# Tile-by-tile ends of two output projections, later S5 set-up in layer 1, and small products ordered behind large ones, in a two-layer decoder trunk

## Chip, cores and metric

The kernel runs on one core of one Trainium2 chip, in one launch. The metric is device microseconds (us) of that core for one execution; the time of a kernel is the median over its runs. Engines are named as in the profile: PE is TensorE (PEld its weight loads), DVE is VectorE, ACT is ScalarE, POOL is GpSimd, SP is SyncE, which here only starts transfers.

## What is computed

The reference runs two layers over x (256 tokens, 1024 channels) and 256 memory tokens, all in float32:

```python
for l in range(2):
    x = x + 0.5 * swiglu(rms_norm(x, ffn1_norm[l]), ...)        # FFN1, width 2816
    h = rms_norm(x, mix_norm[l])
    z = h @ w_in[l]                                             # columns for 4 mixers + 4 gates
    y_a, y_b, y_c, y_d = mlstm(...), s5(...), gla(...), rwkv7(...)
    merged = sum(sigmoid(gate_b) * y_b)                         # per channel
    x = x + merged @ w_out[l]
    x = x + cross_attention(rms_norm(x, xattn_norm[l]), rms_norm(mem, mem_norm[l]))   # ends in @ wo
    x = x + 0.5 * swiglu(rms_norm(x, ffn2_norm[l]), ...)        # FFN2
return rms_norm(x, final_norm)
```

S5 is a complex diagonal state-space model of 32 groups; GLA is gated linear attention with 4 heads, whose scores are built here in eight levels (block sizes 128, 64, ... 1). The rest of the reference is not touched by the change.

## The kernel before

**Layout.** Activations lie transposed, 128 channels on the partitions and 256 tokens along the free axis; `self.x` is 8 such tiles. Each large product is made in float32 out of two rounded parts: weight w is split into hi and lo (`whi`, `wlo`), the activation too (`xhi`, `xlo`), and `mm3` (L256) adds three products hi*hi, hi*lo, lo*hi into PSUM. The FFN's later tiles use `mm2` (L263), one 512-column and one 256-column matmul per block.

**Weights.** `chunk` (L229) fetches 128x1024 halves in the order in which they are first used: a transfer on SP's queue into one of 3 `wraw` buffers, a copy to `whi` on ACT (L244), a subtraction to `wlo` on DVE (L245). There are 4 `whi`/`wlo` buffers; a buffer is free again when its 8 blocks' matmuls (24 of `mm3`) are done.

**Order of the work.** Only SP's queue keeps the order of the program text. The other engines' queues are put in order at build time by a list scheduler that simulates the program: an engine takes, among the instructions that are ready in the simulation, the one that stands first in the text. On the chip each queue then runs strictly in that order, and an instruction that is not ready holds up all behind it. `tc.issue_after(i)` adds the rule that what is written inside the block stands behind instruction i in the queue of i's engine; it adds no wait for i to end.

**FFN1 and S5's set-up.** `ffn` (L396) has 22 steps f (gate and up columns) and 8 steps d (down). In FFN1 it calls `s5_ahead` (L445) after each step with numbers 0 to 29. At the numbers in `S5_AT[layer]` POOL's share of S5's set-up is written (`s5_prep`, L1054, then `s5_mats`, L1152, for tiles 0 to 3: 49 small POOL instructions each, which build Bp and Cp); at the numbers in `S5_PE[layer]` the rest of a tile follows (`s5_finish`, L460): 8 transposes (L1209), 8 products (L1215, two instructions each in the trace), three ACT copies (L1210, L1218), four DVE instructions (L1220) and six transfers on ACT's queue (L1225, L1228).

```python
S5_AT = (2, 6, 11, 17, 22), (3, 8, 13, 18, 22)
S5_PE = (17, 22, 25, 29), (14, 19, 24, 28)
```

**The mixer stage.** `mix` (L647) writes RWKV first and then interleaves four generators by the string `ORDER[layer]`: S is one step of S5, G of GLA, M of mLSTM, D of the dense work (16 gate steps `gps`, 48 matmuls of `mm3` each in two halves of 24, L1576 and L259 to L261, in `gates`, L1564; then the keys and values of the memory). The third G to the tenth are GLA's eight levels: DVE differences (L785, L786), an ACT exponential (L787), three POOL products (L788, L794 or L798), then the score matmuls (L804, L807 or L810) and their copy into A (ACT L814, L817, or DVE L822). `gQ` has two buffers, used by turns. An S5 tile (`s5_tile`, L1254) multiplies into `px` (L1262) and `yps` (L1265), scans on DVE, adds the outputs into `yps` (L1290), then applies its nonlinearity.

**The projections.** `mix_out` (L1624, w_out) and the end of `xattn` (L520, wo) both call `proj_k` (L598) for four input chunks c: for each of 8 output tiles d it adds 6 matmuls into `acc`, and at c = 3 DVE adds the finished tile to `self.x` (L610). The next product's inputs are made from x by `gained` (ACT L343 `xhi`, DVE L344 `xlo`), and its norm from squares (ACT L310, POOL L312). In `xattn` chunk c is head c; `head(3)` is written between chunks 0 and 1.

Of the kernel before, what the change touches and what calls it, by code (L numbers as in the profile page):

```python
# [18 lines left out]
P = 128  # L19
# [5 lines left out]
LAZY = 5, 5  # L25
MEM_AT = 0, 0
S5_AT = (2, 6, 11, 17, 22), (3, 8, 13, 18, 22)
S5_PE = (17, 22, 25, 29), (14, 19, 24, 28)
ORDER = ("SSDSSSDSSSGSDSSGSDSGDGDGDGDGDGDDGDGDGMDGMDGMMDMDMMDMDDDDDD",
         "SSSSSSSSSSSSDSDGDGDGDMGDMGDMGDMGDMGDMGDMGDMGDGDGDDDDDDDDDD")  # L30
POS = 0, 1, 3, 2, 4
# [45 lines left out]
class K:  # L77
# [173 lines left out]
    def split(self, src, hi, lo, scale=None, eng=None):  # L251
        nc = self.nc
        nc.scalar.copy(hi, src)
        (eng or nc.vector).tensor_tensor(lo, src, hi.bitcast(F32), ALU.subtract)

    def mm3(self, ps, w, x, first, last):  # L256

        nc = self.nc
        nc.tensor.matmul(ps, w[0], x[0], start=first, stop=False)  # L259
        nc.tensor.matmul(ps, w[0], x[1], start=False, stop=False)  # L260
        nc.tensor.matmul(ps, w[1], x[0], start=False, stop=last)  # L261

    def mm2(self, ps, w, x, first, last):  # L263

# [255 lines left out]
    def xattn(self):  # L520
        nc, l = self.nc, self.l
        self.pdt = "psd", 2
        if self.kv is None:
            self.mem_gained()
            for _ in self.mem_kv():
                pass
        (kT, v), self.kv = self.kv, None
        self.br = "x"
        hi, lo = self.gained(self.x, "xattn_norm")
        qs, acc = [], [self.px([P, 2, T], "acc", br="o") for _ in range(4)]  # L530

        def q_of(c):
            ps = self.pd("qps")
            self.prod(self.chunk(self.ins["wq"][l, c]), ps, hi, lo, c == 0)
            qT = [self.hp.tile([P, 2, T], F32R, name=self.nm("qT")) for _ in range(2)]
            self.split(ps, *qT)
            qs.append(qT)
        for c in range(2):
            q_of(c)
        y = self.rstd_tok(self.x)  # L540
        rq = self.tp.tile([P, 4], F32, tag="rq", name=self.nm("rq"))
        nc.vector.tensor_scalar(rq[:, 0:2], y, 1.0 / 16, None, ALU.mult)
        nc.vector.tensor_scalar(rq[:, 2:4], y, -1.0 / 16, None, ALU.mult)
        es = [self.softmax(0, qs, rq, kT)]
        q_of(2)
        es.append(self.softmax(1, qs, rq, kT))
        oh = [self.head(0, es[0], v)]
        q_of(3)
        for h in range(2, 4):
            es.append(self.softmax(h, qs, rq, kT))  # L550
            oh.append(self.head(h - 1, es[h - 1], v))
        self.proj_k("wo", 0, *oh[0], acc)
        oh.append(self.head(3, es[3], v))
        for h in range(1, 4):
            self.proj_k("wo", h, *oh[h], acc)

    def softmax(self, h, qs, rq, kT):

# [36 lines left out]
        self.split(ops, hi, lo)  # L595
        return hi, lo

    def proj_k(self, wname, c, hi, lo, acc):  # L598

        nc, l = self.nc, self.l  # L600
        blk = self.chunk(self.ins[wname][l, c])
        for d in range(8):
            ps = acc[d // 2][:, d % 2, :]
            for k in range(2):
                w = blk(2 * d + k)
                for i, (wi, x) in enumerate(((0, hi), (0, lo), (1, hi))):
                    nc.tensor.matmul(ps, w[wi], x[:, k, :], start=(c == 0 and d % 2 == 0 and k == 0 and i == 0),  # L607
                                     stop=(c == 3 and k == 1 and i == 2), skip_group_check=True)
            if c == 3:
                nc.vector.tensor_tensor(self.x[:, d, :], ps, self.x[:, d, :], ALU.add)  # L610


    def ot(self, shape, dt=F32, n="ot", bufs=None):
# [99 lines left out]
    def gla(self):  # L713
        nc, l, sp = self.nc, self.l, self.tp
        self.small_cols()
        ps = self.wtiles(7)
        q = self.ot([P, 2, T], n="cq")
        nc.scalar.mul(q, ps, 0.125)
        ps = self.wtiles(8)
# [3 lines left out]
        for c in range(2):  # L723
            blk = self.chunk(self.ins["cv"][l, c])
            ps = self.pd("vps")
# [12 lines left out]
        ps = self.px([P, 2, T])  # L738
# [13 lines left out]
        b = self.ot([P, 2, T], n="gb")  # L752
# [19 lines left out]
        for tt in range(2):  # L772
            for pr in range(2):
                for par in range(2):
                    c = 4 * tt + 2 * pr + par
                    nc.scalar.mul(A[:, pr, tt, par, :], self.ident, dg[:, c:c + 1])
        yield
        for lv, m in enumerate((128, 64, 32, 16, 8, 4, 2, 1)):
            nb = 2 * T // (2 * m)
            halves = lambda t: f2(t).rearrange("p (n h j) -> p n h j", h=2, j=m)  # L780
            bv = halves(b)
            X = self.ot([P, 2, T], n="gE", bufs=3)
            Xv = halves(X)
            mid = bv[:, :, 0, m - 1:m].to_broadcast([P, nb, m])
            nc.vector.tensor_tensor(Xv[:, :, 0, :], mid, bv[:, :, 0, :], ALU.subtract)  # L785
            nc.vector.tensor_tensor(Xv[:, :, 1, :], bv[:, :, 1, :], mid, ALU.subtract)  # L786
            nc.scalar.activation(X, X, AF.Exp, scale=1.0 / 16)  # L787
            nc.gpsimd.tensor_tensor(Xv[:, :, 0, :], Xv[:, :, 0, :], halves(k)[:, :, 0, :], ALU.mult)  # L788
            Qm = Q[:, lv % 2]
            for par in range(2):  # L790
                r = slice(64 * par, 64 * par + 64)
                if m == 128:
                    second = lambda t: halves(t)[r, :, 1, :].rearrange("p a (g j) -> p a g j", j=64)
                    nc.gpsimd.tensor_tensor(Qm[r, :, par, :].rearrange("p (a g) j -> p a g j", a=2), second(X), second(q),  # L794
                                            ALU.mult)
                else:
                    second = lambda t: halves(t)[r, :, 1, :].rearrange("p (a n) j -> p a n j", a=4)
                    nc.gpsimd.tensor_tensor(Qm[r, :, par, :].rearrange("p a (n j) -> p a n j", j=m), second(X), second(q),  # L798
                                            ALU.mult)
            ps = self.px([P, 4, 2, 64])  # L800
            for c in range(4):
                pr, tt = divmod(c, 2)
                if m == 128:
                    nc.tensor.matmul(ps[:, c], X[:, pr, 0:P], Qm[:, c], start=True, stop=True)  # L804
                elif m >= 32:
                    for n in range(0, P, 2 * m):
                        nc.tensor.matmul(ps[n:n + m, c, :, 0:m], X[:, pr, tt * P + n:tt * P + n + m],  # L807
                                         Qm[:, c, :, n // 2:n // 2 + m], start=True, stop=True)
                else:
                    nc.tensor.matmul(ps[:, c], X[:, pr, tt * P:(tt + 1) * P], Qm[:, c], start=True, stop=True)  # L810
            pu = ps.rearrange("p c a t -> p (c a) t")
            if m == 128:
                for pr in range(2):
                    nc.scalar.copy(Ao[:, pr].rearrange("p a (g t) -> p g a t", t=64), ps[:, 2 * pr:2 * pr + 2])  # L814
            elif m >= 32:
                for n in range(0, P, 2 * m):
                    nc.scalar.copy(Au[n:n + m, :, n + m:n + 2 * m], pu[n:n + m, :, 0:m])  # L817
            else:

                half = lambda ap: ap.rearrange("p (n h j) -> p n h j", h=2, j=m)[:, :, 1, :]  # L820
                mask = half(self.lvl[m].bitcast(I32)).unsqueeze(1).to_broadcast([P, 8, P // (2 * m), m])
                nc.vector.copy_predicated(Au.rearrange("p u (n h j) -> p u n h j", h=2, j=m)[:, :, :, 1, :], mask,  # L822
                                          pu.rearrange("p u (n j) -> p u n j", j=m))
            yield
# [3 lines left out]
        for pr in range(2):  # L828
            ops = self.px([P, 2, T])
            for par in range(2):  # L830
                h = 2 * pr + par
# [5 lines left out]
            for par in range(2):  # L837
                for tt in range(2):
                    sq = ops[:, tt, par * P:(par + 1) * P]
                    c = tt * 4 + 2 * pr + par  # L840
# [12 lines left out]
        for hp in range(2):  # L853
            ps = self.wtiles(9 + hp)
# [4 lines left out]
            for hh in range(2):  # L859
                h = hp * 2 + hh  # L860
# [393 lines left out]
    def s5_tile(self, i, us, y):  # L1254

        nc, l, sp = self.nc, self.l, self.tp
        V = nc.vector.tensor_tensor
        W, In, Cp = self.Wp[i], self.In[i], self.Cp[i]
        w = self.px([P, 2, T])
# [3 lines left out]
        yps = self.px([P, 4, P], n="yps", br="y")[:, :, 0:64]  # L1263
# [21 lines left out]
        ss = a  # L1285
        V(ss[:, 0, :], a[:, 0, :], b[:, 1, :], ALU.subtract)
        V(ss[:, 1, :], a[:, 1, :], b[:, 0, :], ALU.add)
        for j in range(4):
            for ri in range(2):
                nc.tensor.matmul(yps[:, j, 1:64], Cp[:, j, ri].rearrange("p a b -> p (a b)"),  # L1290
                                 ss[:, ri, 64 * j:64 * j + 63], start=False, stop=(ri == 1), skip_group_check=True)
        yield
        th = self.ot([P, T], n="bth", bufs=1)
        tv = th.rearrange("p (j k) -> p j k", k=64)
# [329 lines left out]
    def mix_out(self):  # L1624
        nc, l = self.nc, self.l
        m = self.merged
        self.tap(f"merged_{l}", m)
        acc = [self.px([P, 2, T], "acc", br="o") for _ in range(4)]
        for c in range(4):
            hi = self.ot([P, 2, T], F32R, n="mghi")  # L1630
            lo = self.ot([P, 2, T], F32R, n="mglo")
            sl = slice(2 * c, 2 * c + 2)
            nc.scalar.mul(hi, m[:, sl, :], 0.5)
            nc.vector.scalar_tensor_tensor(lo, m[:, sl, :], 0.5, hi.bitcast(F32), ALU.mult, ALU.subtract)
            self.proj_k("wout", c, hi, lo, acc)


    def final(self):
# [152 lines left out]
```

## Time and profile before

| | |
|---|---|
| median of 3 runs | 1828.23 us (1826.98 to 1835.68) |
| the profiled execution's own time | 1828.79 us |
| its span, first to last instruction | 1827.1 us |
| busy share of the span | PE 97%, PEld 91%, DVE 74%, ACT 53%, POOL 31% |
| mean granted TensorE clock | 0.986 |

A duration in the rows is that of one instruction from start to end; consecutive matmuls overlap, so PE is idle only where the profile shows a gap, with the engine that ended it in brackets. The granted clock is 1.00 at 2.4 GHz and 0.50 at 1.2 GHz.

### The profile page before, as it was taken

How to read it: one execution, taken by the hardware profiler on the slowest of the kernel's cores; microseconds unless marked ns; L12 is line 12 of the kernel's file. 1: busy time of each engine (PE TensorE's matmuls, PEld its weight loads, DVE VectorE, ACT ScalarE, POOL GpSimd, SP SyncE). 2: the span in 40 equal slices, each digit the busy share in tenths (PEclk: the TensorE clock that was granted, in tenths of full speed). 3: DMA queues.
4: the chain of work that ended last, by engine and by line, in shares of the span. 5: the costliest groups of instructions: out<-in, count | busy, mean ns of one | idle time of the engine just before them, and what ended most of it. 6: DMA issues, size and time to landing. Idle time of an engine off the chain costs nothing. (4 is left out here: it accounts for less than half of the span.)

```text
span 1827.1 us, 34052 instructions
## 1 busy us (share of the span) xinstructions
PE 1771.7 (97%) x13156; PEld 1657.4 (91%) x13156; DVE 1343.1 (74%) x2325; ACT 959.6 (53%) x1594; POOL 573.9 (31%) x765
## 2 busy tenths in 40 slices
PE   7999999999999999999999899999999999999997
PEld 7888899889999999988898789999989999999886
DVE  8987678895576876866699666698856667768654
ACT  4665464456454455555456454645555544546552
POOL 4999521170011211200149893113021103111001
PEclk9999999999999999999999899999999999999999
DMA  6575563457346653555557466635444586445553
GB/s 196 169 211 183 187 206 110 138 179 222 115 153 222 227 188 115 180 189 185 183 167 218 139 188 201 201 108 172 164 137 146 186 258 217 149 136 186 185 186 103
DMA packets 131843, 320.16 MB, mean 175 GB/s; under 512 B 45792, under 2 KB 50912, under 8 KB 131168
## 3 DMA queue, kind: packets, MB, share of 16 engines
q1 hardware_dynamic: 83664, 290.31, 49.6%
q10 hardware_dynamic: 48016, 27.67, 5.3%
q8 instruction: 103, 1.69, 0.4%
q14 instruction: 60, 0.49, 0.1%
HBM read 300.11 MB, written 16.52 MB: 173 GB/s over the span
## 5 line engine op out<-in xcount | busy, mean ns | idle before, releaser
L245 DVE TENSOR_TENSOR wlo<-wraw,whi 128x1024 fp32r<-128x1024 f32 x524 | 677.8, 1295 | 315.7 <-ACT whi L244 310.1
L244 ACT CAST whi<-wraw 128x1024 fp32r<-128x1024 f32 x524 | 547.2, 1048 | 575.7 <-issue 103.3
L266 PE MATMUL gu<-hl,whi 128*128 128x512 f32 x1024 | 363.4, 399 | 0.0
L267 PE MATMUL gu<-hl,wlo 128*128 128x256 f32 x1024 | 288.5, 282 | 0.4 <-DVE wlo L245 0.4
L266 PE MATMUL dn<-ahl,whi 128*128 128x512 f32 x704 | 248.4, 397 | 0.0
L266 PEld LDWEIGHTS gu<-hl,whi 128*128 128x128 f32 x1024 | 193.0, 189 | 47.5
L312 POOL TENSOR_TENSOR arena<-arena 128x256 f32<-128x256 f32 x69 | 75.2, 1090 | 483.2 <-ACT arena L310 480.3
L267 PE MATMUL dn<-ahl,wlo 128*128 128x256 f32 x704 | 197.2, 281 | 0.8 <-DVE wlo L245 0.8
L267 PEld LDWEIGHTS gu<-hl,wlo 128*128 128x128 f32 x1024 | 194.1, 190 | 0.9 <-DVE wlo L245 0.9
L266 PEld LDWEIGHTS dn<-ahl,whi 128*128 128x128 f32 x704 | 131.9, 188 | 31.6
L259 PE MATMUL gps<-hhi,whi 128*128 128x256 f32 x512 | 153.2, 299 | 6.2 <-ACT gst L1576 5.8
L260 PE MATMUL gps<-hlo,whi 128*128 128x256 f32 x512 | 150.5, 294 | 0.0
L261 PE MATMUL gps<-hhi,wlo 128*128 128x256 f32 x512 | 149.5, 293 | 0.8 <-DVE wlo L245 0.8
L267 PEld LDWEIGHTS dn<-ahl,wlo 128*128 128x128 f32 x704 | 133.0, 189 | 1.4 <-DVE wlo L245 1.1
L259 PE MATMUL zin<-hhi,whi 128*128 128x256 f32 x384 | 111.6, 291 | 2.4 <-ACT gst L1576 2.4
L260 PE MATMUL zin<-hlo,whi 128*128 128x256 f32 x384 | 110.5, 288 | 0.0
L259 PEld LDWEIGHTS gps<-hhi,whi 128*128 128x128 f32 x512 | 102.1, 199 | 9.2 <-ACT gst L1576 6.7
L261 PE MATMUL zin<-hhi,wlo 128*128 128x256 f32 x384 | 110.2, 287 | 0.0
L260 PEld LDWEIGHTS gps<-hlo,whi 128*128 128x128 f32 x512 | 101.9, 199 | 2.3 <-issue 2.0
L261 PEld LDWEIGHTS gps<-hhi,wlo 128*128 128x128 f32 x512 | 101.5, 199 | 1.7 <-DVE wlo L245 1.0
L261 PE MATMUL gu<-xhi,wlo 128*128 128x256 f32 x320 | 91.3, 285 | 0.1
L259 PE MATMUL gu<-xhi,whi 128*128 128x256 f32 x320 | 91.3, 285 | 0.0
(535 smaller groups left out, 4622.2 us busy)
## 6 DMA issues: line engine op xcount, KB each, us to landing
wraw<-in_gu_dram SPq DMA_DIRECT2D x176, 512.0 KB, 3.7
wraw<-in_dn_dram SPq DMA_DIRECT2D x88, 512.0 KB, 3.5
wraw<-in_win_dram SPq DMA_DIRECT2D x68, 512.0 KB, 4.0
wraw<-in_gates_dram SPq DMA_DIRECT2D x64, 512.0 KB, 4.2
gd<-gst ACTq DMA_DIRECT2D x32, 256.0 KB, 2.1
wraw<-in_wk_dram SPq DMA_DIRECT2D x16, 512.0 KB, 3.8
wraw<-in_wv_dram SPq DMA_DIRECT2D x16, 512.0 KB, 3.5
gld<-gd SPq DMA_DIRECT2D x32, 256.0 KB, 4.2
```

The source lines that it names most:

```text
L244: nc.scalar.copy(hi, raw)
L245: nc.vector.tensor_tensor(lo, raw, hi.bitcast(F32), ALU.subtract)
L259: nc.tensor.matmul(ps, w[0], x[0], start=first, stop=False)
L260: nc.tensor.matmul(ps, w[0], x[1], start=False, stop=False)
L261: nc.tensor.matmul(ps, w[1], x[0], start=False, stop=last)
L266: nc.tensor.matmul(ps, w[0], x, start=first, stop=False, skip_group_check=True)
L267: nc.tensor.matmul(ps[:, 1, :], w[1], x[:, 0, :], start=False, stop=last, skip_group_check=True)
L312: nc.gpsimd.tensor_tensor(acc, acc, sq, ALU.add)
```

## The change

It does four things. `proj_last` takes chunks 2 and 3 of both projections together, so that each output tile gets its last 12 matmuls and is then finished; c = 0 and c = 1 stay as they were. `S5_PE` of layer 1 moves the four `s5_finish` calls from 14, 19, 24, 28 to 17, 22, 26, 29. GLA's score matmuls and S5's output matmuls are put behind `self.large`, the last matmul of `mm3` written before them. `mix_out` makes all four input parts before the last two chunks.

```diff
-S5_PE = (17, 22, 25, 29), (14, 19, 24, 28)
+S5_PE = (17, 22, 25, 29), (17, 22, 26, 29)
...
+    def behind(self):
+
+        return self.tc.issue_after(self.large.ins)
+
     def mm3(self, ps, w, x, first, last):
...
-        nc.tensor.matmul(ps, w[1], x[0], start=False, stop=last)
+        self.large = nc.tensor.matmul(ps, w[1], x[0], start=False, stop=last)
...
         oh.append(self.head(3, es[3], v))
-        for h in range(1, 4):
-            self.proj_k("wo", h, *oh[h], acc)
+        self.proj_k("wo", 1, *oh[1], acc)
+        self.proj_last("wo", oh[2], oh[3], acc)
...
-    def proj_k(self, wname, c, hi, lo, acc):
+    def proj_k(self, wname, c, hi, lo, acc, ds=range(8), blk=None):
 
         nc, l = self.nc, self.l
-        blk = self.chunk(self.ins[wname][l, c])
-        for d in range(8):
+        blk = blk or self.chunk(self.ins[wname][l, c])
+        for d in ds:
...
+    def proj_last(self, wname, x2, x3, acc):
+
+        blks = [self.chunk(self.ins[wname][self.l, c]) for c in (2, 3)]
+        for d in range(8):
+            for c, x in ((2, x2), (3, x3)):
+                self.proj_k(wname, c, *x, acc, (d,), blks[c - 2])
...
             ps = self.px([P, 4, 2, 64])
-            for c in range(4):
...
+            with self.behind():
+                for c in range(4):
...
-        for j in range(4):
-            for ri in range(2):
-                nc.tensor.matmul(yps[:, j, 1:64], Cp[:, j, ri].rearrange("p a b -> p (a b)"),
-                                 ss[:, ri, 64 * j:64 * j + 63], start=False, stop=(ri == 1), skip_group_check=True)
+        with self.behind():
+            for j in range(4):
+                for ri in range(2):
+                    nc.tensor.matmul(yps[:, j, 1:64], Cp[:, j, ri].rearrange("p a b -> p (a b)"),
+                                     ss[:, ri, 64 * j:64 * j + 63], start=False, stop=(ri == 1), skip_group_check=True)
...
         acc = [self.px([P, 2, T], "acc", br="o") for _ in range(4)]
+        parts = []
         for c in range(4):
...
-            self.proj_k("wout", c, hi, lo, acc)
+            parts.append((hi, lo))
+            if c < 2:
+                self.proj_k("wout", c, hi, lo, acc)
+        self.proj_last("wout", *parts[2:], acc)
```

## Rows read from the trace of the kernel before

**Rows 1.** The page's first part: busy time, share of the span and instructions of each engine.

```profile
PE 1771.7 (97%) x13156; PEld 1657.4 (91%) x13156; DVE 1343.1 (74%) x2325; ACT 959.6 (53%) x1594; POOL 573.9 (31%) x765
```

**Rows 2.** PE's waits over the whole span: us in total, times, longest.

```profile
PE wps L1209 <- POOL s5Bp L1179: 7.8, 1, 7.8
...
PE gps L259 <- ACT gst L1576: 5.8, 5, 3.2
...
PE qps L261 <- DVE wlo L245: 1.9, 2, 1.0
...
PE qps L372 <- DVE xlo L344: 1.3, 4, 0.4
```

**Rows 3.** Windows: a plain FFN step; tile 0's stretch, layers 1, 0: busy, PEclk, DMA.

```profile
996.19:1001.84 5.65, 5.65 (x34) 4.79 (x32) 5.39 (x9) 3.27 (x6) 5.65 (x8) 1.00 0.90 280
1001.84:1020.40 18.56, 10.73 (x58) 8.96 (x57) 8.84 (x8) 2.58 (x5) 18.56 (x46) 0.72 0.22 66
121.43:129.21 7.78, 7.78 (x59) 6.79 (x57) 6.16 (x12) 4.12 (x9) 7.78 (x14) 1.00 0.73 189
```

**Rows 4.** PE's timeline: transposes of tiles 0 and 1 (layer 0), tile 0 (layer 1).

```profile
121.43 0.60 PE L1209 MATMUL wps<-consts,s5Bp 128*128 128x128 f32 x4
...
153.13 0.60 PE L1209 MATMUL wps<-consts,s5Bp 128*128 128x128 f32 x4
...
1009.82 1.32 PE L1209 MATMUL wps<-consts,s5Bp 128*128 128x128 f32 x4 [7.83 <-POOL s5Bp L1179]
```

**Rows 5.** POOL's timeline: first instruction and last memset of set-up tiles, both layers.

```profile
80.62 1.39 POOL L1187 TENSOR_TENSOR bu<-s5Bp,arena 128x128 f32<-128x128 f32 x1
...
116.48 0.52 POOL L1201 MEMSET s5box<- 128x512 f32 x1
...
147.09 0.52 POOL L1201 MEMSET s5box<- 128x512 f32 x1
...
979.31 1.39 POOL L1187 TENSOR_TENSOR bu<-s5Bp,arena 128x128 f32<-128x128 f32 x1
...
1043.25 0.40 POOL L1187 TENSOR_TENSOR bu<-s5Bp,arena 128x128 f32<-128x128 f32 x1 [7.61 <-DMA s5Bp<-in_s_bc_dram]
```

**Rows 6.** Timeline, layer 1: first matmul of w_out on PE, its last input part on DVE.

```profile
1534.57 0.28 PE L607 MATMUL acc<-mghi,whi 128*128 128x256 f32 x1
...
1543.14 0.68 DVE L1634 SCALAR_TENSOR_TENSOR mglo<-merged,mghi 128x512 fp32r<-128x512 f32 x1
```

**Rows 7.** PE's waits at the start of FFN2, windows 720 to 735 and 1620 to 1632.

```profile
PE gu L372 <- DVE xlo L344: 1.5, 2, 1.2
...
PE gu L372 <- DVE xlo L344: 1.2, 1, 1.2
```

**Rows 8.** DVE's timeline at the end of wo, layer 1: head 3's part, first finished tile.

```profile
1615.24 0.68 DVE L254 TENSOR_TENSOR olo<-ops,ohi 128x512 fp32r<-128x512 f32 x1
1618.13 0.43 DVE L610 TENSOR_TENSOR x<-acc,x 128x256 f32<-128x256 f32 x1 [2.21 <-PE acc L607]
```

**Rows 9.** Windows, columns as in rows 3: after wo (layer 1); GLA's levels (layer 0).

```profile
1626.90:1630.30 3.40, 3.40 (x19) 3.40 (x18) 3.15 (x3) 0.47 (x2) 3.17 (x4) 0.50 0.29 73
...
391.99:394.51 2.52, 0.00 (x2) 0.00 (x1) 2.49 (x5) 1.94 (x3) 2.46 (x1) 1.00 0.00 0
394.60:398.10 3.50, 3.50 (x17) 3.50 (x18) 3.43 (x5) 0.42 (x1) 3.42 (x3) 0.51 0.93 268
...
376.00:412.00 36.00, 32.15 (x264) 31.48 (x264) 35.42 (x53) 16.26 (x29) 25.03 (x20) 0.95 0.56 186
```

**Rows 10.** Gate matmuls (one of three) before L807's last group, L810's end, layer 1's L804.

```profile
L259 PE MATMUL gps<-hhi,whi 128*128 128x256 f32 x88 | 27.4, 311 | 3.2 <-ACT gst L1576 3.2
...
L259 PE MATMUL gps<-hhi,whi 128*128 128x256 f32 x160 | 49.3, 308 | 4.6 <-ACT gst L1576 4.6
...
L259 PE MATMUL gps<-hhi,whi 128*128 128x256 f32 x56 | 17.4, 310 | 0.0
```

**Rows 11.** PE's group of score matmuls of levels 3 to 7, window 376 to 412.

```profile
L810 PE MATMUL px<-gQ,gE 128*128 128x128 f32 x38 | 6.0, 283 | 2.5 <-POOL gQ L798 2.5
```

More of the change, by code (lines that the diff above doesn't have):

```diff
@@ L800, in gla @@
             ps = self.px([P, 4, 2, 64])
-            for c in range(4):
[L802 to L810, printed above, removed]
+            with self.behind():
+                for c in range(4):
+                    pr, tt = divmod(c, 2)
+                    if m == 128:
+                        nc.tensor.matmul(ps[:, c], X[:, pr, 0:P], Qm[:, c], start=True, stop=True)
+                    elif m >= 32:
+                        for n in range(0, P, 2 * m):
+                            nc.tensor.matmul(ps[n:n + m, c, :, 0:m], X[:, pr, tt * P + n:tt * P + n + m],
+                                             Qm[:, c, :, n // 2:n // 2 + m], start=True, stop=True)
+                    else:
+                        nc.tensor.matmul(ps[:, c], X[:, pr, tt * P:(tt + 1) * P], Qm[:, c], start=True, stop=True)
             pu = ps.rearrange("p c a t -> p (c a) t")
```

## The prediction, made before the changed kernel was run

> **What bounds the kernel now.** I read the page's busy shares first: PE is busy 97% of the span [rows 1], so the time is the sum of PE's work and of what holds it up. PE's waits come next [rows 2]. Leaving out the start and the end of the kernel, which the change does not touch, the list is short: one wait of 7.8 us for POOL in S5's set-up, 5.8 us in five waits of gate products for ACT, 3.2 us at the first query product (1.9 + 1.3), 2.5 us for POOL at GLA's scores [rows 11], and 2.7 us at FFN2's start [rows 7]. Then I looked at the windows for the granted clock: after a wait it falls to 0.50 for some us [rows 9], so a wait costs more than its own length. No instruction of PE disappears with this change, and none is added. Everything it can win is in these waits and the clock behind them.
>
> The sum is made against the profiled execution's 1828.8 us. The median of the runs is 0.6 us lower, and I take that off at the end. About 0.5% (9.1 us) is what a measurement of this kernel can tell from no change.
>
> **S5's set-up in layer 1.** The transposes of tile 0 stand behind step 14 and wait 7.83 us for POOL [rows 4]. The same work in layer 0 stands behind step 17 and does not wait. From tile 0's place to the start of the second FFN step after it, PE issues the same instructions in both layers (58 and 59 recorded), in 7.78 us at full clock in layer 0 and in 18.56 us at a mean clock of 0.72 in layer 1 [rows 3]. The difference, 10.8 us, is wait and half clock together. With 17 for 14, layer 1 has layer 0's place.
>
> Is POOL done by then? In layer 0 tile 0 took POOL from 80.62 to 116.48, 35.9 us, and PE came at 121.43, 4.9 us later [rows 4, 5]. In layer 1 POOL starts at 979.31, so by layer 0's pace it ends at 1015.2. PE would arrive three steps after 1001.84. A plain step is 5.65 us [rows 3], so it comes at 1018.8, 3.6 us after POOL. Tile 1 follows POOL in layer 0 by 6.0 us (147.09, 153.13) [rows 4, 5]. In layer 1 it takes POOL to 1015.2 + 30.6 = 1045.8, and PE comes at step 22, near 1051. Tile 2 waits in layer 1 for its input transfer, 7.61 us [rows 5]. That transfer is issued behind step 18, and steps now come 10.8 us sooner, so it lands before POOL is free at 1045.8. Tiles 2 and 3 then have eight us and more. The three copies on ACT, the four instructions on DVE and the six transfers on ACT's queue move along with each tile, past the weight copies of three FFN steps; they are inside layer 0's 7.78 us. I take **10.8 us**. Above it lies the same with a little of the mixer's first waits covered by tile 3's work, 11.6; below it the wait comes back in part, which is a rival.
>
> One rule speaks against this. The rows show the same POOL instruction at 1.39 us and at 0.40 us [rows 5]. During the wait DVE had little to do (8.84 us busy in 18.56) [rows 3], and POOL ran at its short times. The Trainium skill, "SBUF — State Buffer", section "Who interferes with whom", says that a DVE instruction with two SBUF inputs and a GpSimd instruction that reads SBUF exclude each other, the later one blocking. By that rule the chain that ended at 1009.8 was quick only because PE's wait had starved DVE, and it will be slower once the wait is gone; layer 0 shows by how much, 35.9 us, and that is the pace taken above.
>
> **The end of w_out, two layers.** A matmul of a dense product takes 0.12 us of PE (264 in 32.15 us [rows 9]). Chunk 2 starts 96 matmuls after 1534.57, so at 1546.1, and the last input part is ready at 1543.8 [rows 6]. So nothing is late for the interleaved order, and the tiles are finished 1.44 us apart from 1547.6 on, where they came 0.72 us apart in the last 5.8 us. DVE's adds (0.43 us each [rows 8]), the `xlo` and the next `wlo` then spread over 11.5 us. The price: two weight buffers come free together 5.8 us before the end instead of one at 8.6 and one at 5.8. A half needs about a microsecond of ACT and one of DVE, so I estimate that two of them are still ready in time. Of 3.2 us of waits over both layers [rows 2] I take back **3.0 us**; bounds 0 and 3.2.
>
> **The end of wo, two layers.** Here the last part is late: head 3's `olo` is done at 1615.9 [rows 8], when 70 of 192 matmuls are still to come. While it is missing, PE takes what is ready, which is the rest of chunk 2. So the order is tile by tile only in part, and the first tile is ready about 1 us earlier than now, not 5. DVE stands 2.21 us before its first add [rows 8] and can use that. Of 2.7 us of waits [rows 7] I take 2.0, and of the half clock behind the one in layer 1 (3.40 us at 0.50, so 1.7 us lost) [rows 9] I take 1.0, since a shorter wait may or may not spare it: **3.0 us**. Bounds: 4.4 if all goes, and 3.0 lost if PE stands for head 3's split (0.68 us on DVE [rows 8], an estimated as much on ACT before it: 1.5 us per layer).
>
> **S5's outputs and GLA's scores.** What binds can be counted. In ORDER[0] the levels 0 to 7 are written behind 4, 5, 6, 7, 8, 9, 11 and 12 gate steps. On PE the last group of L807 (level 2) now comes after 88 x 3 / 48 = 5.5 steps and the last of L810 after 10.0 [rows 10]; so levels 2 to 7 move back by half a step to two steps. In ORDER[1] level 0 is written behind 4 steps and now comes after 3.5 [rows 10]; I take the later levels and S5's outputs as already standing where the rule wants them, and cost them at nothing: they would be PE work beside other PE work.
>
> In layer 0 the 2.52 us wait for POOL goes, because 24 gate matmuls and more come first (2.9 us). With the 3.50 us at half clock behind it [rows 9] it is worth 4.3 us at most. But in that stretch DVE is the next limit: it was busy 2.49 of the 2.52 us, and 35.4 of 36 us from 376 to 412 [rows 9]. It makes the `wlo` of each half product, so PE cannot run far ahead, and about 38 score matmuls (0.11 us apart at the least, with the turn-overs between groups some 5 us by estimate) [rows 11] move out of the stretch into one where PE is full. I take **1.5 us**, between 4.3 gained and 5 lost, near neither end since both happen in part. The gate products' waits for ACT stay: ACT's own queue sets them.
>
> Sum: 10.8 + 3.0 + 3.0 + 1.5 = 18.3 us. 1828.8 - 18.3 = 1810.5 in the profiled execution's terms, **1810 us** as a median.
>
> **The rivals.**
> 1. *Only the set-up pays.* Head 3 keeps wo's end late, DVE keeps the gate stretch, and w_out's end turns its waits into others. For it speaks DVE's 98% in the window; against it that w_out's parts are all early. 1828.2 - 10.8 = 1817 to 1818.
> 2. *The set-up's wait comes back.* POOL is blocked more by DVE than in layer 0: 10% slower uses up the 3.6 us. The rule above is this rival's mechanism, and layer 0's own rows, under a full DVE, speak against it. If 7.8 us return with their clock, about 9 of the 10.8 are lost: 1819.
> 3. *The scores do not move.* If PE's queue has them behind the gate steps anyway, or the levels just swap places, that part is 0: 1812.
> 4. *Slower.* The scores become a standing queue. Each of the six moved levels in layer 0 and the one in layer 1 now stands at the head of PE's queue with no gate product before it that could fill the time, and each waits as the one at 391.99 did, 2.52 us and 1.75 us of clock. Seven such waits are 30 us against the 16.8 of the other parts: 1841. From four waits on the change gains nothing. Against it: a gate step takes 48 x 0.12 = 5.8 us of PE, and POOL was busy 25.0 us of 36 [rows 9] over some five levels, 5 us each.
>
> **How the numbers follow.** The forecast has 0.55, with a range of its own from 1803 to 1817; rival 1 has 0.22, rival 2 0.08, rival 3 0.11, rival 4 0.04. Forecast and rival 3 lie beyond 9.1 us; rival 1 sits just beyond (10.8) and goes a little more than half to faster; rival 2 mostly to the same. Faster 0.80, same 0.15, slower 0.05. The range runs from 1801 (all upper bounds: 11.6 + 3.2 + 4.4 + 4.3 = 23.5 us, and a few us from waits that I left alone) to 1824 (10.8 less the lower bounds of wo and the scores, 10.8 - 3 - 5 = 2.8).
>
> **What would show it.** In the profile after: no wait of L1209 for POOL over 1 us, and tile 0's stretch in layer 1 near 7.8 us at clock 1.00; DVE's L610 of w_out 1.4 us apart and no `qps` wait over 0.3 us; L810's last group after 12 gate steps in layer 0 and no wait for `gQ`; PE's idle time at some 40 us of the span, where it is 55.4 now. A wait of L1209 at steps 17 or 22, `acc` waiting for `ohi` or `olo`, or L804 to L810 waiting for `gQ` at several levels would make it wrong.

## The result, and the profile after

The change makes the kernel slower: 1841.62 us against 1827.76 us, a ratio of 1.0078 (95% interval 1.0061 to 1.0095), so 14 us longer. Forecast were 18 us less.

The first fence has the page's busy shares (compare [rows 1]), the second PE's waits over the whole span: us in total, times, longest. L1209 is L1221 now, L1482 is L1495, L810 is L822.

```profile
PE 1781.1 (97%) x13156; PEld 1666.9 (90%) x13156; DVE 1335.0 (72%) x2325; ACT 957.2 (52%) x1594; POOL 583.8 (32%) x765
```

```profile
PE gps L263 <- ACT gst L1589: 11.4, 5, 3.8
PE px L1495 <- DMA Tw<-dW: 8.0, 2, 4.0
...
PE dn L271 <- DVE wlo L245: 5.3, 2, 4.6
...
PE yps L1303 <- DVE ba L1298: 2.8, 1, 2.8
...
PE acc L611 <- ACT ohi L253: 1.8, 4, 0.7
...
PE qps L376 <- DVE xlo L348: 1.2, 5, 0.3
```

The span grew by 14.8 us, from 1827.1 to 1841.9. PE was idle 5.4 us longer (60.8 for 55.4), and the same 13156 matmuls kept it busy 9.4 us longer, at a mean granted clock of 0.979 for 0.986.

The waits that the forecast wanted gone are gone [rows 2]: POOL's 7.8 us at `wps`, the `wlo` part (1.9 us) of the query product's, POOL's 2.5 us at the scores. Others stand in their place: gate products for ACT 11.4 us where it was 5.8 (8.2 with the `zin` products that waited for the same ACT copy), `Tw` 8.0 where it was 1.7, the down product 5.3 where it was 0.8, and S5's output 2.8 where there was none.

Where the time went is read from three windows: layer 0's mixer, FFN1 of layer 1 and layer 1's mixer, each from its first matmul to the next stage's. A row has the stretch and its length, the busy us (and instructions) of PE, PEld, DVE, ACT and POOL, the granted clock, DMA's share and GB/s. The kernel before comes first.

```profile
215.02:636.20 421.18, 412.57 (x3474) 399.99 (x3473) 315.74 (x564) 219.21 (x363) 92.23 (x80) 0.98 0.55 177
915.53:1121.78 206.25, 198.43 (x1259) 177.16 (x1258) 162.51 (x275) 107.78 (x179) 161.29 (x249) 0.98 0.59 179
1121.78:1534.57 412.79, 406.89 (x3463) 394.99 (x3461) 305.07 (x546) 216.91 (x351) 75.07 (x73) 0.99 0.55 177
```

After the change there follow the same three, tile 0's stretch in layer 1, and pairs of a wait and the half clock that came with it:

```profile
216.07:643.46 427.39, 416.04 (x3475) 403.36 (x3474) 312.88 (x563) 219.95 (x363) 90.35 (x80) 0.97 0.54 175
921.82:1125.19 203.37, 198.81 (x1254) 177.21 (x1252) 161.92 (x274) 106.99 (x179) 163.13 (x249) 0.98 0.58 181
1125.19:1549.31 424.12, 412.51 (x3466) 400.89 (x3465) 298.56 (x548) 215.58 (x353) 81.12 (x73) 0.97 0.54 172
...
1025.10:1032.88 7.78, 7.78 (x59) 6.79 (x58) 5.90 (x11) 4.58 (x9) 7.78 (x15) 1.00 0.53 153
1102.44:1106.99 4.55, 0.01 (x1) 0.00 (x0) 4.47 (x6) 0.33 (x1) 3.28 (x6) 0.93 0.03 7
1106.30:1113.20 6.90, 6.19 (x20) 5.33 (x21) 3.86 (x5) 3.10 (x4) 0.00 (x0) 0.51 0.75 188
428.01:431.99 3.98, 0.00 (x0) 0.00 (x1) 1.23 (x1) 1.52 (x2) 0.00 (x0) 0.81 1.10 271
430.50:440.70 10.20, 8.71 (x85) 8.19 (x85) 1.48 (x2) 3.68 (x6) 0.00 (x0) 0.50 0.51 161
1201.82:1204.59 2.77, 0.00 (x1) 0.00 (x0) 2.77 (x8) 0.00 (x0) 0.00 (x0) 1.00 0.00 0
1205.30:1215.60 10.30, 10.30 (x50) 10.15 (x50) 9.61 (x28) 1.16 (x3) 0.00 (x0) 0.50 0.36 113
...
361.23:364.41 3.18, 0.01 (x1) 0.01 (x1) 3.18 (x11) 3.13 (x5) 0.00 (x0) 1.00 0.00 0
365.70:369.10 3.40, 3.40 (x18) 3.40 (x17) 3.30 (x6) 3.38 (x7) 3.25 (x4) 0.50 0.42 154
```

Layer 0's mixer is 6.2 us longer and layer 1's 11.3. FFN1 of layer 1 is only 2.9 us shorter, although tile 0's stretch takes 7.78 us at full clock for the 18.56 of before [rows 3]. These three make up 14.7 of the 14.8 us, so in this pair of profiles all other stages, the ends of both projections among them, brought nothing. The timeline shows what stands at the waits:

```profile
431.99 1.22 PE L1495 MATMUL px<-Tw,L 32*32 32x32 f32 x19 [3.98 <-DMA Tw<-dW]
...
1025.10 0.60 PE L1221 MATMUL wps<-consts,s5Bp 128*128 128x128 f32 x4
...
1098.23 0.42 ACT L314 ACTIVATE arena<-x 128x256 f32<-128x256 f32 x1 [6.29 <-POOL arena L316]
...
1099.08 4.33 DVE L348 SCALAR_TENSOR_TENSOR xlo<-x,consts,xhi 128x256 fp32r<-128x256 f32 x1 [7.17 <-ACT xhi L347]
...
1103.08 0.51 POOL L1213 MEMSET s5box<- 128x512 f32 x1
...
1105.31 1.64 DVE L245 TENSOR_TENSOR wlo<-wraw,whi 128x1024 fp32r<-128x1024 f32 x1
...
1107.01 0.58 PE L271 MATMUL dn<-ahl,wlo 128*128 128x256 f32 x1 [4.56 <-DVE wlo L245]
...
1204.60 0.43 PE L1303 MATMUL yps<-ba,s5box 128*128 128x63 f32 x2 [2.77 <-DVE ba L1298]
```

In FFN1's down part ACT's square of a finished tile (L314) waits for a buffer that POOL's sum (L316) frees. That sum stands in POOL's queue among tile 3's set-up, which ends with the memset at 1103.1. ACT's weight copies stand behind the square. DVE's subtraction that makes `wlo` (1105.31) stands behind `xlo`, and PE waits for that `wlo`. In layer 1's mixer S5's first output product waits for DVE's scan. In the kernel before, 24 gate products stood ahead of it, and it did not wait:

```profile
1204.69 0.28 PE L261 MATMUL gps<-hhi,wlo 128*128 128x256 f32 x1
...
1206.66 0.61 PE L1290 MATMUL yps<-ba,s5box 128*128 128x63 f32 x4
```

### The profile page after: what moved, and what is told of

It is laid out like the page before. It is cut to its first block, busy times and chain, and to the rows that moved or that the text cites. A ratio compares the mean times of both kernels' runs of the same rounds, so it can differ in the third digit from the quotient of the medians.

```text
span 1841.9 us, 34046 instructions
## 1 busy us (share of the span) xinstructions
PE 1781.1 (97%) x13156; PEld 1666.9 (90%) x13156; DVE 1335.0 (72%) x2325; ACT 957.2 (52%) x1594; POOL 583.8 (32%) x765
## 4 chain that ended last, share of the span: by engine, by line
PE 68%; POOL 17%; DVE 6%; DMA 4%; ACT 3%; issue 3%; ACTq 1%; POOLq 0%; SPq 0%; DVEq 0%
PE gu L270 7%; PE dn L270 5%; PE gu L271 3%; PE acc L611 3%; PE zin L263 3%; PE zin L264 3%; PE zin L265 3%; PE dn L271 3%; PE gps L263 2%; PE gps L264 2%; PE gps L265 2%; DVE wlo L245 2%; POOL bu L1189 2%; PE gu L265 2%; PE gu L264 2%
## 5 line engine op out<-in xcount | busy, mean ns | idle before, releaser
L270 PE MATMUL dn<-ahl,whi 128*128 128x512 f32 x704 | 252.2, 402 | 1.1 <-ACT whi L244 1.1
L316 POOL TENSOR_TENSOR arena<-arena 128x256 f32<-128x256 f32 x69 | 74.9, 1086 | 488.4 <-ACT arena L314 485.5
L263 PE MATMUL gps<-hhi,whi 128*128 128x256 f32 x512 | 155.0, 303 | 11.5 <-ACT gst L1589 11.4
L263 PEld LDWEIGHTS gps<-hhi,whi 128*128 128x128 f32 x512 | 103.5, 202 | 14.7 <-ACT gst L1589 12.7
```

What stands on the lines that cost most here:

```text
L270: nc.tensor.matmul(ps, w[0], x, start=first, stop=False, skip_group_check=True)
L316: nc.gpsimd.tensor_tensor(acc, acc, sq, ALU.add)
```

## The experiments

All variants start from the kernel before. The ratio is to that kernel, timed beside the variant, with its 95% interval. In the cuts of code the lines taken out are those of the changed kernel; in e7's cut they are those of the kernel before.

| | what | median, us | ratio |
|---|---|---|---|
| e1 | S5_PE alone | 1831.47 | 1.0025 (1.0009 to 1.0041) |
| e2 | w_out alone | 1835.10 | 1.0048 (1.0031 to 1.0064) |
| e3 | wo alone | 1823.59 | 0.9991 (0.9978 to 1.0005) |
| e4 | scores alone | 1837.03 | 1.0058 (1.0042 to 1.0075) |
| e5 | w_out, layer 1 | 1823.77 | 0.9997 (0.9982 to 1.0012) |
| e6 | w_out, layer 0 | 1838.59 | 1.0079 (1.0054 to 1.0103) |
| e7 | S5_PE, tile 3 at 28 | 1824.62 | 1.0000 (0.9986 to 1.0015) |
| e8 | e7, POOL one step sooner | 1821.68 | 0.9984 (0.9971 to 0.9997) |
| e9 | e7, own buffers for squares | 1827.26 | 1.0004 (0.9990 to 1.0019) |
| e10 | scores, layer 0 | 1832.12 | 1.0033 (1.0015 to 1.0052) |
| e11 | e10, last levels free | 1825.37 | 0.9998 (0.9981 to 1.0015) |
| e12 | e7, sum on DVE | 1816.31 | 0.9953 (0.9938 to 0.9968) |
| e13 | sum on DVE alone | 1823.91 | 0.9988 (0.9972 to 1.0003) |
| e14 | e12 and e5 | 1813.49 | 0.9946 (0.9925 to 0.9967) |

### One part at a time: e1 to e4

e1 has the changed line `S5_PE` alone, e2 `mix_out` alone, e3 the lines of `xattn` alone, e4 `with self.behind()` at the scores alone. The fifth part needs no run of its own: the kernel before with the rule at S5's outputs alone builds to the same program as without it, byte for byte.

> The kernel before with S5_PE of layer 1 alone changed to (17, 22, 26, 29). Theory (what arrives early is handed back): the transposes of tile 0 no longer wait, -11 to -13 us by the first product of the down part; then PE meets POOL's work on tile 3 while POOL is still at it, a weight copy on DVE is late by 4 to 5 us and the down part of FFN1 grows by 8 to 10 us; and the shifted instructions re-sort the queues of layer 1's mixer: the output products of S5's tile 0 stand ahead of a gate step and not behind it, wait for DVE's scan (some 2.8 us and 10 us at half clock), +8 to +11 us in the mixer. Sum: 1834 us (1829 to 1840). Rival 1, the forecast (the set-up's gain stays): 1817. Rival 2 (the loss in layer 1's mixer is from the rule of standing behind large products): the down part gives 8 to 10 back, the mixer nothing, 1825.

> The kernel before with the tile-by-tile end of w_out alone. Theory: w_out and the query product behind it are 1.2 us shorter in layer 0 and 0.8 us in layer 1; layer 1's mixer has its queues re-sorted, but S5's outputs of tile 0 stay behind a gate step, so it costs 0 to 3 us there: 1826 to 1829. Rival 1, the forecast's term: -3.0, 1825. Rival 2 (any re-sorting of layer 1's mixer costs what the whole change lost there): +8 to +11 there, 1834 to 1837.

> The kernel before with the tile-by-tile end of wo alone. Theory: PE stands for head 3's parts (0.7 us) and still for xlo and wlo at FFN2's start (1.3 us), what the 1.8 us of waits at FFN2's start were: 0 to +1 us per layer, 1828 to 1829. Rival, the forecast's term: -3.0, 1825.

> The kernel before with GLA's score products behind the large products alone. Theory: in layer 0 the wait for POOL at the scores goes, PE runs ahead with gate products, and stands for RWKV's transfer into Tw instead (4 us and 10 us at half clock for 0.3 us and 3.4 us before): +6 us in layer 0's mixer; layer 1 +0 to +4: 1834 (1831 to 1839). Rival 1, the forecast's term: -1.5, 1826. Rival 2 (layer 0's loss belongs to something else in the whole change): 1828.

Against 1825.66 us, e1 costs 4.6 us (0.25%), e2 8.8 and e4 10.6. e3 gives 1.6 us, with an interval from 4.0 gained to 0.9 lost: that cannot be told from nothing, nor from the forecast's 3.0. For e1 and e4 the theory's sign and mechanism hold, though e1's mixer lost less than the 8 to 11 us expected, and e4 is heavier than layer 0 alone explains. For e2 the theory was wrong and its second rival's time right. The parts sum to 22 us and the whole change costs 14, so they do not add up. Three of them change the same thing, the order of PE's queue in layer 1's mixer. e1's windows of FFN1 and the mixer, and its output product:

```profile
915.39:1118.84 203.45, 198.84 (x1255) 177.12 (x1253) 162.16 (x274) 106.96 (x179) 163.21 (x249) 0.98 0.55 181
1118.84:1535.96 417.12, 410.12 (x3466) 398.23 (x3465) 301.50 (x548) 215.97 (x353) 78.99 (x73) 0.98 0.52 175
```

```profile
1197.89 0.43 PE L1303 MATMUL yps<-ba,s5box 128*128 128x63 f32 x2 [2.48 <-DVE ba L1298]
```

### Is it the edit or the order of layer 1's mixer? e5, e6, e7

```diff
-            if c < 2:
-                self.proj_k("wout", c, hi, lo, acc)
-        self.proj_last("wout", *parts[2:], acc)
+            if c < 2 or l != 1:
+                self.proj_k("wout", c, hi, lo, acc)
+        if l == 1:
+            self.proj_last("wout", *parts[2:], acc)
```

e6 is the same with 0 for 1. e7 has e1's line with tile 3 left at 28:

```diff
-S5_PE = (17, 22, 25, 29), (14, 19, 24, 28)
+S5_PE = (17, 22, 25, 29), (17, 22, 26, 28)
```

> The kernel before with the tile-by-tile end of w_out in layer 1 alone. Theory (the edit itself pays, and what it cost in e2 comes from layer 1's mixer, whose queues the build re-sorts when the work ahead of it changes): nothing behind layer 1's w_out can re-sort the mixer ahead of it, so only the 0.7 to 1.0 us at the query product is left: -1 us, 1823 to 1827 beside 1825.7 of the kernel before. Rival (the end of w_out itself costs, in the projection or later): half of e2's loss, +4 us or more.

> The kernel before with the tile-by-tile end of w_out in layer 0 alone. Theory: layer 1's mixer has the same order on PE as in e2, so the whole loss of e2 is here: layer 0's w_out and query product -1.2 us, layer 1's mixer +8 to +11 us with 3 us of waits for weight copies of zin products and more half clock: +8 us, 1832 to 1836. Rival (e2's loss lies in the edit's two places): +4 us or less.

> The kernel before with S5_PE of layer 1 at (17, 22, 26, 28): tile 3 stays where it was, and with it the order on PE in layer 1's mixer is that of the kernel before. Theory: FFN1 of layer 1 as in e1 (-13 us at the set-up, +8 to +10 us back in the down part, where POOL is still at tile 3), the mixer as before: -3 us, 1820 to 1825. Rival 1 (e1's mixer loss came from arriving early, not from the order): +4 us as e1, 1829 to 1832. Rival 2 (the down part's loss came from tile 3's place at 29): -11 to -13 us, 1813 to 1816.

e5 came out as the theory has it: in layer 1 the new end of w_out costs nothing that can be told (-0.5 us). e6 came out in place and sign, but larger than the 8 us expected: in layer 0 the same edit costs 14 us, with an interval from 10 to 19 (e2, with the same order of PE in layer 1's mixer, 9). The loss is not where the edit is. Layer 1's mixer, which starts 460 us later, takes 425.56 us, with PE waiting for a weight subtraction and three stretches at half clock. e6's windows, the mixer and those stretches:

```profile
1118.70:1544.26 425.56, 416.50 (x3463) 403.10 (x3462) 301.55 (x546) 216.95 (x351) 75.88 (x73) 0.97 0.52 172
...
1244.10:1254.40 10.30, 10.30 (x46) 9.40 (x45) 5.24 (x10) 5.25 (x13) 0.83 (x1) 0.50 0.25 79
1288.50:1295.30 6.80, 6.04 (x28) 6.05 (x29) 5.34 (x13) 1.27 (x2) 0.00 (x0) 0.50 0.67 231
1353.40:1363.60 10.20, 10.20 (x62) 9.22 (x60) 2.08 (x6) 2.79 (x9) 1.04 (x3) 0.50 0.15 51
```

e7 leaves that order alone, and its time is that of the kernel before; of the 3 us that its theory expected it shows none. Its mixer takes 409.06 us, its FFN1 203.86, much as e1's.

```profile
916.25:1120.11 203.86, 199.30 (x1259) 177.58 (x1257) 161.96 (x278) 107.14 (x179) 162.48 (x249) 0.98 0.56 182
1120.11:1529.17 409.06, 403.99 (x3463) 392.05 (x3461) 306.17 (x546) 216.17 (x351) 74.46 (x73) 1.00 0.53 179
```

So moving tile 3 from 28 to 29 makes the 0.25% between e1 and e7 (which is little more than the noise of the two ratios together), through the order of a later stage. One profiled mixer says less than the ratios: with PE's order of the kernel before, layer 1's took from 406.16 us (e10) to 412.79 (the kernel before itself) in seven profiles. In e11 to e14, where a few instructions stand elsewhere, it took 405.40 to 409.74. Widely re-sorted it took 416.60 (e4) to 425.56 (e6) in five. So the groups do not overlap, and the 11.3 us above are measured from the slowest of the first.

### What takes the set-up's gain back? e8, e9, e12, e13

e8 sets `S5_AT` of layer 1 to (2, 7, 12, 17, 21). e9 gives the squares of the norm behind FFN1 of layer 1 tiles of their own. e12 lets DVE add them:

```diff
-                nc.gpsimd.tensor_tensor(acc, acc, sq, ALU.add)
+                (nc.vector if self.on_dve else nc.gpsimd).tensor_tensor(acc, acc, sq, ALU.add)
...
-            self.rs = self.rstd_row(self.x)
+            self.on_dve = l == 1; self.rs = self.rstd_row(self.x); self.on_dve = False
```

> As e7, and POOL's share starts one FFN step sooner (S5_AT of layer 1 at (2, 7, 12, 17, 21)); the mixer's order on PE is that of the kernel before. Theory (what returns the set-up's gain is that POOL's tile 3 ends late against PE): POOL is done with tile 3 some 5 us sooner than in e1's 1096.7, the wait for the weight copy (4.6 us and its half clock) goes or halves, the down part is 66 to 71 us for e1's 75.8: -8 to -12 us, 1814 to 1818. Rival 1 (POOL and DVE collide in the down part wherever tile 3 lies): down part 74 to 76, as e7. Rival 2 (POOL is late through its input transfers, so nothing moves): as e7, 1820 to 1825.

> As e7, and the squares of the norm behind FFN1 of layer 1 get a buffer each in place of a ring of three. Theory (in the down part ACT's square of the third finished tile waits 6.3 us for a buffer that POOL frees only behind its work on tile 3, and the weight copies stand behind that square in ACT's queue): ACT waits no more, PE's wait for a weight copy (4.6 us, then 6.8 us at half clock) goes, the down part falls from 76 to 66 to 69 us: -8 to -11 us, 1814 to 1817 beside 1824.3. Rival 1 (the long DVE instruction of 4.3 us beside POOL's unbroken run is what starves PE): the down part stays at 72 to 76, 1821 to 1825. Rival 2 (the wait turns up at the norm's end, as the sum on POOL is as late as before): the down part is short, and the first mixer products wait for the norm, 1820 to 1824.

> As e7, and the sum of the squares behind FFN1 of layer 1 is added on DVE instead of POOL (7 instructions of some 0.4 us). In e9 the squares' own buffers lay in memory that still waited for POOL, so that ACT's wait grew to 15.5 us and the down part to 80.1; this takes POOL out of the chain. Theory (ACT's square waits for POOL's sums, which stand behind tile 3 in POOL's queue, and the weight copies stand behind the square): the down part falls from 76 to 66 to 68 us, FFN1 of layer 1 is 8 to 11 us shorter in all than in the kernel before: 1814 to 1819 beside 1825 of the kernel before. Rival (DVE held off by POOL's unbroken run is the cause): the down part stays at 71 to 76, 1821 to 1825.

> The kernel before with that sum on DVE alone, S5_PE as it was: what of e12 is the sum itself. Theory: in the kernel before PE does not wait in the down part (65.4 us), so nothing moves: -1 to +1 us, 1824 to 1826. Rival (the sum on DVE shortens the norm or frees POOL, whatever S5_PE is): -3 us or more.

The square on ACT in e7, in e8 (with the end of tile 3 on POOL) and in e9 (with PE's wait):

```profile
1092.66 0.42 ACT L314 ACTIVATE arena<-x 128x256 f32<-128x256 f32 x1 [6.28 <-POOL arena L316]
```

```profile
1097.32 0.42 ACT L314 ACTIVATE arena<-x 128x256 f32<-128x256 f32 x1 [10.01 <-POOL arena L316]
...
1098.05 0.53 POOL L1213 MEMSET s5box<- 128x512 f32 x1
```

```profile
1088.62 0.42 ACT L314 ACTIVATE sq<-x 128x256 f32<-128x256 f32 x1 [15.49 <-POOL arena L316]
...
1090.43 0.80 PE L270 MATMUL dn<-ahl,whi 128*128 128x512 f32 x1 [7.00 <-ACT whi L244]
```

e8's theory fell: POOL was no sooner done (1098.05), FFN1 took 203.60 us, and 2.9 us were gained where 8 to 12 were expected. So did e9's: the new tiles did not free ACT, its square still waited for POOL's sum, and longer, and FFN1 took 207.78 us. The rival is DVE's long `xlo`. In the changed kernel and in e7 it took 4.33 us right ahead of the `wlo` that PE waited for, and by estimate 3.7 us of PE's 4.56 come from its length beyond 0.62. But the loss does not need it: in e8 and e9 it took 0.48 and 0.62 us, ACT's square waited 10.01 and 15.49 us in place of 6.28, and FFN1 was as long or longer. What the runs share is the square's wait for POOL's sum, and e12 takes that away. PE does not wait in the down part at all there, and FFN1 takes 196.85 us (then the mixer's row, and e13's FFN1):

```profile
913.08:1109.93 196.85, 196.77 (x1259) 175.39 (x1257) 158.94 (x281) 107.42 (x179) 163.92 (x243) 1.00 0.57 188
...
1109.93:1517.22 407.29, 403.82 (x3462) 392.05 (x3461) 303.84 (x547) 216.45 (x351) 75.59 (x72) 1.00 0.54 179
...
918.72:1124.58 205.86, 198.04 (x1259) 176.53 (x1257) 165.54 (x284) 108.23 (x179) 156.11 (x243) 0.98 0.55 181
```

The sum on DVE alone (e13) is worth 2.2 us by its ratio, and its interval takes in none; FFN1 has 205.86 us there for 206.25. With the set-up moved (e12 against e7) it is worth 0.47%, 8.6 us, and FFN1 is 7.0 us shorter.

### The scores in layer 0: e10, e11

```diff
-            with self.behind():
+            with self.behind() if l == 0 and m >= 4 else self.tc.issue_after(self.normed.ins):
```

e10 is without `and m >= 4`; `m` is a level's block size. `self.normed` is an instruction of POOL, so the other branch binds nothing on PE.

> The kernel before with GLA's score products behind the large products in layer 0 alone; layer 1's mixer has the order of the kernel before on PE. Theory: the whole of +6 us of layer 0's mixer is here, with a wait of 3 to 4 us for Tw and some 10 us at half clock behind it: 1829 to 1832 beside 1824.3. Rival (layer 0's mixer differs by as much from run to run): 1823 to 1826.

> As e10, but the last levels (block sizes 2 and 1) may stand where they are ready. On PE their scores and the 12 products after them then come ahead of RWKV's products with Tw, as in the kernel before; a few S5 outputs of layer 1 stand elsewhere. Theory (layer 0 loses because work that filled PE until Tw lands has moved behind it): the wait for Tw is under 1.5 us, the 10 us at half clock are gone, layer 0's mixer is 420 to 423 us for e10's 427. Rival (RWKV's chain on DVE is late by the rule itself, so Tw is late whatever stands ahead of it): 425 to 428.

RWKV's product with `Tw` in the kernel before, with two of the matmuls at half clock behind it; then layer 0's mixer and that product in e10 and in e11:

```profile
428.64 1.66 PE L1482 MATMUL px<-Tw,L 32*32 32x32 f32 x64 [0.27 <-DMA Tw<-dW]
...
432.61 0.41 PE L260 MATMUL gps<-hlo,whi 128*128 128x256 f32 x1
432.83 0.41 PE L261 MATMUL gps<-hhi,wlo 128*128 128x256 f32 x1
```

```profile
215.74:643.40 427.66, 414.18 (x3474) 401.53 (x3473) 311.82 (x561) 218.11 (x362) 92.94 (x80) 0.97 0.53 173
```

```profile
432.01 1.91 PE L1495 MATMUL px<-Tw,L 32*32 32x32 f32 x32 [3.17 <-DMA Tw<-dW]
```

```profile
215.08:635.75 420.67, 410.80 (x3474) 398.50 (x3473) 316.13 (x564) 219.90 (x363) 89.25 (x80) 0.98 0.53 178
```

```profile
431.92 2.25 PE L1495 MATMUL px<-Tw,L 32*32 32x32 f32 x64 [0.70 <-DMA Tw<-dW]
```

`Tw` is there at the same time in both, near 432, and 3.3 us later than in the kernel before; why it is later with the rule was not traced. In e11 PE has the last two levels and GLA's value products to do until then; in e10 they stand behind. So the loss comes from having nothing left to do while `Tw` is on its way, and not from a late `Tw` alone. The profiled mixers of layer 0 agree: 426.96 to 427.66 us in the three kernels with the whole rule, and 419.42 to 421.53 in eleven of the twelve without it (425.11 in e13). e11 gains nothing either: without the wait for `gQ` its layer 0 mixer takes 420.67 us for 421.18.

The other 4.6 us of e4 (0.58% less 0.33%) are about as large as the noise of the two ratios together. The profiles put them into layer 1's mixer, where the rule moves the order from level 0 on, in e4 and then in e10:

```profile
1127.44:1544.04 416.60, 409.10 (x3462) 396.80 (x3461) 301.11 (x546) 215.91 (x351) 77.95 (x73) 0.98 0.53 175
...
1128.42:1534.58 406.16, 402.21 (x3462) 390.46 (x3461) 304.32 (x546) 216.05 (x351) 76.42 (x73) 1.00 0.54 180
```

### Together: e14

> e12 with the tile-by-tile end of w_out in layer 1 (e5). Theory: e12's time less 0 to 1 us, 1813 to 1818, below both kernels. Rival: as e7, 1821 to 1825.

1813.49 us is 0.54% below the kernel before, and by the two ratios (0.9946 / 1.0078) 1.3% below the changed one. That it beats e12 is within the intervals.

## Why the prediction was wrong

**Where the 33 us lie.** The forecast was 18.3 us gained, and in the two profiles the change lost 14.8. Of the 33.1 us between them, 7.9 are the set-up's (10.8 taken, FFN1 2.9 shorter), 11.3 layer 1's mixer (nothing taken), 7.7 the scores in layer 0 (1.5 taken, 6.2 lost), and 6.1 the two projections' ends with all that is left (6.0 taken).

**The set-up.** Its own numbers held. In e1 POOL's last memset of tile 0 began at 1013.8 (forecast 1015.2), PE came at 1018.7 (1018.8), and tile 0's stretch took layer 0's 7.78 us. The step that failed is the claim that what moves along lies inside those 7.78 us, and with it the whole 10.8: POOL's own work was timed against PE's set-up products only, not against what else is queued on POOL. PE now reaches the down part while POOL is still at tile 3, and the norm's sums stand in that queue. FFN1 gained 2.4 us in e7 in place of 10.8, and 9.4 in e12, where the sums were out of the way.

**The order of the other stages.** The sum took every stage that the diff does not name as unchanged. The build's list scheduler does not keep them so: tile 3 at 29 (e1), and w_out's end in layer 0 (e6), each re-sorted layer 1's mixer, for 0.25% and 0.79%. No term or rival had this, and it is the largest miss.

**w_out's end.** 2.0 of 3.2 us of waits went (the 1.9 us for `wlo` and 0.1 of the 1.3 for `xlo`), where 3.0 were taken. The mechanism was right, and the size was off. That those 2.0 us shorten the kernel is not shown: e5's ratio, which has layer 1's half of it, cannot be told from nothing (3.3 us gained to 2.2 lost).

**wo's end.** The lower bound's mechanism came: PE stands for head 3's parts, 0.9 us per layer (1.8 in all, where 0.5 stood before), and still 0.6 to 0.7 us each for `xlo` and `wlo`. One reading was off: 58 of wo's matmuls, not 70, come after head 3's `olo` in the trace. The term of 3.0 us is 1.6 by e3's ratio, whose interval (4.0 gained to 0.9 lost) holds both 3.0 and nothing.

**The scores.** The wait for `gQ` went, as forecast, but 1.5 us gained became 6.0 lost in layer 0 (e10, with an interval from 2.7 to 9.5, against a bound of 5). The failing step is that the scores "move out of the stretch into one where PE is full": the last two levels moved behind RWKV's product, and PE stood 3.2 us for `Tw` without them. For layer 1, level 0 alone was thought to move; the later levels moved too. The gate products' waits for ACT, which were to stay, went from 5.8 to 7.3 us in layer 0. But they are 9.3 in e13, which has the order of the kernel before there, so that this comes from the change is not shown.

**S5's outputs.** The rule by itself changes nothing, as forecast. The wait at them comes with e1's re-sorting, 2.48 us there without the rule.

**The rivals.** Rival 4 gave 1841 and the median is 1841.6, but by chance: no scores wait for `gQ`. Its time lay outside the range, whose end of 1824 is also 1.4 us under what its own terms give (1828.2 - 2.8 = 1825.4). Rival 2, the set-up's wait itself, did not come. Its mechanism shows elsewhere: DVE's `xlo`, which reads `x` and `xhi`, takes 4.33 us beside an unbroken run of POOL and 0.62 in the kernel before. The Trainium skill, "SBUF — State Buffer", section "Who interferes with whom", says that a DVE instruction with two SBUF inputs contends with a GpSimd instruction that reads SBUF, and the trace agrees. It lengthened PE's wait in the down part, but e8 shows the same loss without it.

**Open.** That the re-sorted mixer is slower is shown, and its waits are read from the traces, but the loss is not traced to one displaced instruction. Why an edit in layer 0 changes the order in layer 1 was not tried.

## What to carry to other kernels

When a wait is removed, list what stands in the queue of the engine that was waited for, and ask which other engines need it when the waiting engine comes early. With a scheduler that sorts by its own simulated times, compare the queues of the whole program before costing an edit as local. Small products that fill PE while a transfer is on its way hide the wait for it. Before a rule moves them back, work out when the next thing that PE will meet arrives.

## What the hardware showed unexpectedly

The half clock's length does not follow the wait's. With 3.18 us of waiting came 3.4 us at 0.50, with 4.55 us 6.9 (the first 0.7 still in the wait), with 3.98 us 10.2 (the first 1.5 still in the wait), but with 2.77 us 10.3. Gate matmuls start 0.21 us apart at half clock (432.61 and 432.83 in the kernel before) and 0.12 at full, so by estimate 4.5 of the 10.3 us are lost, more than the 2.77 of the wait itself. By the same estimate the 8.7 us behind the wait of 3.98 lose 3.8, about as much as the wait.

One DVE instruction of 0.62 us in the kernel before took 4.33 while POOL ran without a gap.
